# First layer's projections: context by itself, then five pairs of blocks as seven half-products

## The chip, the cores and the metric

One core of a Trainium2 chip runs the whole program. The time is that of the device for one execution, in microseconds (us); three runs were made of the kernel before, and one further execution was recorded by the profiler. TensorE (PE in the rows) multiplies matrices, ScalarE (ACT), VectorE (DVE) and GpSimd (POOL) work element by element, and SyncE (SP) and GpSimd issue the DMA transfers.

## The reference

Two layers of a backbone over 1024 latent tokens and 256 context tokens, width 1024. Each layer normalises and modulates its input, projects it with one matrix of 1024 x 3,488 columns, runs four groups on the parts (neighbourhood attention, latent attention with low rank, a token MLP, a short convolution), gates each, projects back and adds:

```python
hx = modulate(rms_norm(x, norm_g), sh_x, sc_x)        # latent, 1024 tokens
hc = modulate(rms_norm(ctx, norm_g), sh_c, sc_c)      # context, 256 tokens
(a_q, a_k, a_v, a_g, b_cq, b_ckv, b_kr, b_g,
 c_u, c_v, c_g, d_b, d_c, d_h, d_g) = jnp.split(hx @ w_in, IN_SPLIT_POINTS, axis=-1)
...
x_new = x + g_x * merge_branches((out_a, out_b, out_c, out_d), (a_g, b_g, c_g, d_g), w_out)
```

Context goes through the same weights. The last layer needs of context only the keys and values (`update_ctx` is false there). All is in float32.

## The kernel before

**Tiles.** Activations lie with channels on the partitions. Tokens come in three chunks (`CHUNKS`, L34): 0 and 1 are the latent tokens, 512 each, and 2 is context, 256. A projection block is 128 output columns; `BLOCKS` (L44) names them, two to most parts: cu, cg (token MLP), dc, dh, db, dg (convolution), ckv0, cq, ak, aq, bg, ag. A product in float32 is made of three matmuls in a faster format: every operand is split into a high part (a cast) and a low part (the rest), and `mm3` (L186) multiplies high by high, high by low, low by high. So a block over one chunk is 8 x 3 = 24 matmuls. Its weights come through `w_block` (L372): a DMA into a tile "wr", the cast on ScalarE into "wh" (L360), the subtraction on GpSimd into "wl" (L365). Each of the three tags has two tiles (`BUFS`, L122); "x" has 20, "g" 24.

**Order.** Code runs once to record instructions. A planner then orders each engine's instructions by when they are ready in its own estimate and by the order in which they were recorded, and gives out tiles as they come free. Between `pe.chain(True)` and `pe.chain(False)` TensorE's instructions keep their recorded order.

**Layer 0** uses `standard()` (L755): every block over all three chunks, with `proj` (L458), from cg to bg; then `ag` (L885) with the first parts of the latent attention (`mla_load`, `mla_keys`, `units[0].prep`) in between (L1437). After each `proj` one of the fillers runs, which compute the conditioning of both layers on VectorE (`mod_group_dve`, L331).

**Layer 1** uses `paired()` (L810). Two blocks of a part and the two latent chunks make a 2 x 2 by 2 x 2 product of half-blocks (4 of the 8 row groups each), computed with seven products in place of eight (`proj2`, L707; `product`, L698, is 12 matmuls of 512 columns). The sums of right-hand tiles are made once, on GpSimd and VectorE (`right_parts` L682, `right_sums` L691). The sums of weights are made for each pair, and each of the seven is split by `w_op` (L674) into one of four tiles, two "wh" and two "wl". The keys and values of context come before, in fixed order, with `av_tile` (L545) for the values and `ckv_steps` (L563) for the low-rank part.

## Time and profile before

| | |
|---|---|
| three runs | median 1477.39 us (1474.11 to 1480.54) |
| profiled execution | 1475.18 us, its span 1473.4 us |
| TensorE (matmul) | 1392.8 us busy, 95% of the span |
| TensorE (weight load) | 1170.5 us, 79% |
| VectorE | 860.6 us, 58% |
| ScalarE | 612.8 us, 42% |
| GpSimd | 499.3 us, 34% |
| granted TensorE clock, mean | 0.992 of full speed |
| DMA | 166.45 MB, mean 113 GB/s |

An engine's share is its busy time over the span. Matmuls overlap each other's ends, so the spacing of their starts tells more than their durations. The granted clock is 1.00 at 2.4 GHz and 0.50 at 1.2 GHz. Layer 0's projections run from about 25 to 448 us, its attention and output to about 815 us; layer 1's projections run to about 1141 us.

### The profile page before, as it was taken

How to read it: one execution, taken by the hardware profiler on the slowest of the kernel's cores; microseconds unless marked ns; L12 is line 12 of the kernel's file. 1: busy time of each engine (PE TensorE's matmuls, PEld its weight loads, DVE VectorE, ACT ScalarE, POOL GpSimd, SP SyncE). 2: the span in 40 equal slices, each digit the busy share in tenths (PEclk: the TensorE clock that was granted, in tenths of full speed). 3: DMA queues.
4: the chain of work that ended last, by engine and by line, in shares of the span. 5: the costliest groups of instructions: out<-in, count | busy, mean ns of one | idle time of the engine just before them, and what ended most of it. 6: DMA issues, size and time to landing. Idle time of an engine off the chain costs nothing. (4 is left out here: it accounts for less than half of the span.)

```text
span 1473.4 us, 23094 instructions
## 1 busy us (share of the span) xinstructions
PE 1392.8 (95%) x8844; PEld 1170.5 (79%) x8844; DVE 860.6 (58%) x1906; ACT 612.8 (42%) x1387; POOL 499.3 (34%) x403
## 2 busy tenths in 40 slices
PE   4999999999998999989999979989998999989997
PEld 2788888988887877678888869768886777778887
DVE  5966648064016777574564647666644777665574
ACT  5611111131226656563443413433443666555533
POOL 2154334032220000546613384633425001065641
PEclk9999999999999999999999999999999999999999
DMA  9513324355542002955433202420438102286241
GB/s 355 197 39 130 111 91 158 113 176 173 162 107 37 1 23 83 173 150 162 143 108 118 72 8 87 136 83 22 157 131 192 21 22 59 93 173 168 84 142 59
DMA packets 83822, 166.45 MB, mean 113 GB/s; under 512 B 8448, under 2 KB 35072, under 8 KB 83584
## 3 DMA queue, kind: packets, MB, share of 16 engines
q1 hardware_dynamic: 66688, 136.66, 28.0%
q0 software_dynamic: 15936, 27.27, 9.3%
q8 instruction: 69, 1.13, 0.3%
q10 hardware_dynamic: 1088, 1.05, 0.2%
q14 instruction: 41, 0.34, 0.1%
HBM read 135.33 MB, written 33.82 MB: 115 GB/s over the span
## 5 line engine op out<-in xcount | busy, mean ns | idle before, releaser
L173 PE MATMUL psb<-g,wh 128*128 128x512 f32 (+1 forms) x2152 | 582.1, 367 | 7.1 <-ACT tmp L730 1.5
L173 PEld LDWEIGHTS psb<-g,wh 128*128 128x128 f32 x2152 | 384.2, 189 | 81.8 <-ACT tmp L730 2.4
L173 PE MATMUL psb<-g,wl 128*128 128x512 f32 (+1 forms) x1256 | 414.8, 372 | 12.2 <-POOL wl L365 8.7
L173 PEld LDWEIGHTS psb<-g,wl 128*128 128x128 f32 x1256 | 237.7, 190 | 57.0 <-POOL wl L365 10.0
L365 POOL TENSOR_TENSOR wl<-wr,wh 128x1024 fp32r<-128x1024 f32 (+2 forms) x46 | 109.9, 2391 | 192.3 <-ACT wh L360 191.2
L173 PE MATMUL psb<-g,st 128*128 128x512 f32 (+1 forms) x616 | 161.2, 378 | 9.2 <-ACT wl L1063 3.7
L1046 DVE TENSOR_REDUCE s<-psb 128x1 f32<-128x512 f32 (+1 forms) x200 | 117.4, 590 | 68.5 <-PE psb L173 66.4
L173 PE MATMUL psb<-g,g 128*128 128x256 f32 (+1 forms) x784 | 129.1, 305 | 3.8 <-DMA g<-scr_ck 1.4
L173 PEld LDWEIGHTS psb<-g,st 128*128 128x128 f32 x616 | 97.0, 190 | 33.0 <-ACT g L1063 6.6
L173 PE MATMUL psv<-pt,g 128*64 128x256 f32 (+1 forms) x1312 | 119.4, 331 | 0.6 <-ACT pt L937 0.5
L937 ACT COPY pt<-pst 128x512 f32<-128x512 f32 x116 | 67.9, 586 | 110.7 <-PE pst L176 109.8
L173 PEld LDWEIGHTS psb<-g,g 128*128 128x128 f32 x784 | 105.2, 191 | 10.9 <-issue 2.9
L340 DVE CUSTOM_DVE_ANT_0 tmp<-g,x 128x512 f32<-128x512 f32 x112 | 94.4, 892 | 22.0 <-POOL x L473 20.3
L173 PEld LDWEIGHTS psv<-pt,g 128*64 128x64 f32 x1312 | 79.3, 137 | 32.4 <-issue 8.5
L176 PE MATMUL pst<-ident,g 128*128 128x128 f32 x448 | 79.1, 278 | 12.4 <-ACT g L1193 7.5
L935 DVE COPY pt<-pst 128x512 f32<-128x512 f32 x116 | 79.1, 683 | 10.3 <-PE pst L176 9.6
L360 ACT CAST wh<-wr 128x1024 fp32r<-128x1024 f32 (+2 forms) x47 | 43.2, 924 | 99.7 <-PE psb L173 70.2
L362 POOL TENSOR_SCALAR wh<-wr 128x1024 fp32r<-128x1024 f32 x16 | 44.4, 2772 | 106.5 <-PE pst L176 65.0
L1379 DVE SCALAR_TENSOR_TENSOR x<-psb,modG,x 128x512 f32<-128x512 f32 (+1 forms) x48 | 29.5, 615 | 85.7 <-PE psb L173 45.0
L176 PEld LDWEIGHTS pst<-ident,g 128*128 128x128 f32 x448 | 54.1, 140 | 29.5 <-ACT g L1193 10.3
L218 POOL TENSOR_TENSOR s<-s,mhalf 128x4 f32<-128x4 f32 (+4 forms) x22 | 35.1, 1595 | 80.9 <-DVE s L278 39.5
L1063 ACT ACTIVATE g<-psb,s,rq 128x512 f32<-128x512 f32 x64 | 49.2, 774 | 20.4 <-DVE s L1058 20.3
(246 smaller groups left out, 2142.3 us busy)
## 6 DMA issues: line engine op xcount, KB each, us to landing
g<-in_wmod SPq DMA_DIRECT2D x48, 512.0 KB, 4.7
wr<-in_wtb SPq DMA_DIRECT2D x28, 512.0 KB, 3.9
wr<-in_wout SPq DMA_DIRECT2D x27, 512.0 KB, 3.8
x<-in_wtb SPq DMA_DIRECT2D x40, 256.0 KB, 4.4
st<-in_nab SPq DMA_DIRECT2D x24, 384.0 KB, 3.4
x<-in_xT SPq DMA_DIRECT2D x32, 256.0 KB, 5.1
g<-scr_q POOLq DMA_DIRECT2D x32, 256.0 KB, 7.2
x<-x SPq DMA_DIRECT2D x24, 256.0 KB, 2.4
```

What stands on the lines that cost most here:

```text
L173: return self._next(nc.tensor.matmul(*p, **k))
L176: return self._next(nc.tensor.transpose(*p, **k))
L218: pool.tensor_tensor(r0, v, mhalf[:, :n], ALU.pow)
L340: dve.tensor_tensor_reduce(junk, w[:, hf * 512:hf * 512 + 512], crow[cond, hf], 1.0, 0.0, ALU.mult, ALU.add, part[:, i, cond, hf:hf + 1])
L360: act.copy(hi, raw)
L362: pool.tensor_scalar(hi, raw, 1.0, None, ALU.mult)
L365: (pool if lo_eng == "pool" else dve).tensor_tensor(lo, raw, f(hi), ALU.subtract)
L935: dve.tensor_copy(dst, src)
L937: act.copy(dst, src)
L1046: dve.reduce_max(st["mx"][:, i:i + 1], s_, AX.X)
L1063: act.activation(dst, sps[i], AF.Exp, bias=nb[:, 1:2], scale=rq[:, 0, tq:tq + 1], accum_out=self.rs[:, t, h, i:i + 1])
L1379: dve.scalar_tensor_tensor(xa, p, mod[l]["G"][:, fb, cond:cond + 1], xa, ALU.mult, ALU.add)
```

## The change

Layer 0 now runs `half_paired()`: `first_groups()` (the old code for cg, dc, dh, db, dg), then `value_blocks`, then five pairs by `proj2`: cq, ak, aq, bg and, after the branch of both layers, ag. `value_blocks` keeps a fixed order on TensorE: `ckv0` over chunks 2 and 1; the ten blocks cq, ak, aq, bg, ag over context alone, each with its own `w_block`; the values of context; `ckv0` over chunk 0; then the values of the latent tokens with the right-hand sums between them. `w_op` takes its tiles from three tags (six tiles) up to bg, and the differences of weights then lie in "x" instead of "wr". In `proj2` further work may be put ahead of any of its products (`mid`): in the last pair, ag, which now has a fixed order too, the loads of the latent attention stand ahead of the second product and its first keys ahead of the seventh; the preparation of the first queries comes after all seven. In layer 1 the weights of ak0 and ckv0 are asked for ahead of the tokens of chunk 1. Five of layer 0's fillers move up, so that all run in `first_groups`. In the neighbourhood attention one transposed tile in three is always copied by VectorE (for even `cb` it was ScalarE), and the context queries there lie in a tile "wr" instead of "st".

```diff
@@ -462,8 +462,9 @@
                 evac(c, p)
-            if fillers:
-                fillers.pop(0)()
+            for _ in range(2 if name in ("dc0", "db0", "dc1", "db1", "dg1") else 1):
+                if fillers:
+                    fillers.pop(0)()
@@ -528,9 +529,13 @@
         wcv = early.get(l) or w_tok(a["wcv"][l], 256)
+        ahead_w = {}
         for c in all_chunks:
             if l > 0:
                 cu(c)
+            if last and c == 1:
+                for n in ("ak0", "ckv0"):
+                    ahead_w[n] = w_block(a["wtb"][l, BLOCKS.index(n)])
             cv_tokens(c)
...
@@ -670,9 +675,10 @@
         nop = [0]
+        w_tags = ["wh", "wl", "wr"]
         def w_op(raw, lo_eng="pool"):
-            t = T(("wh", "wl")[nop[0] % 2], [2, 512], F32R)
+            t = T(w_tags[nop[0] % len(w_tags)], [2, 512], F32R)
             nop[0] += 1
@@ -704,55 +710,66 @@
-        def proj2(base, evac, mid=None):
+        def proj2(base, evac, mid={}, raw="x"):
             r = {}
             for j in range(2):
+                t = T("st", [2, 512]) if raw == "st" else None
                 for k in range(2):
-                    r[j, k] = T("x", [512])
+                    r[j, k] = T("x", [512]) if t is None else t[:, k]
                     sp.dma_start(r[j, k], a["wtb"][l, BLOCKS.index(f"{base}{j}")][:, k * 512:(k + 1) * 512])
-            q = T("wr", [2, 512])
+            qt = T("wr", [2, 512]) if "wr" not in w_tags else None
+            q = [T("x", [512]) if qt is None else qt[:, k] for k in range(2)]
             a11, a12 = w_op(r[0, 0]), w_op(r[0, 1])
-            dve.tensor_tensor(q[:, 1, :], r[0, 0], r[1, 0], ALU.subtract)
+            dve.tensor_tensor(q[1], r[0, 0], r[1, 0], ALU.subtract)
             dve.tensor_tensor(r[1, 0], r[1, 0], r[1, 1], ALU.add)
-            dve.tensor_tensor(q[:, 0, :], r[1, 0], r[0, 0], ALU.subtract)
-            dve.tensor_tensor(r[0, 1], r[0, 1], q[:, 0, :], ALU.subtract)
-            s2, s1 = w_op(q[:, 0, :], "dve"), w_op(r[1, 0])
-            x_, y_ = PS("b", [512]), PS("b", [512])
-            product(x_, a11, "11")
-            m1 = T("tmp", [512])
-            act.copy(m1, x_)
-            product(y_, a12, "21")
+            dve.tensor_tensor(q[0], r[1, 0], r[0, 0], ALU.subtract)
+            dve.tensor_tensor(r[0, 1], r[0, 1], q[0], ALU.subtract)
+            ops = {0: a11, 1: a12, 2: w_op(q[0], "dve"), 3: w_op(r[1, 0])}
+            later = {0: (4, q[1], "dve"), 2: (5, r[0, 1], "dve"), 3: (6, r[1, 1], "pool")}
+            x_, y_, z_ = PS("b", [512]), None, None
+            def step(n, p, name, first=True):
+                for fn in mid.get(n, []):
+                    fn()
+                product(p, ops[n], name, first)
+                if n in later:
+                    k, src, eng = later[n]
+                    ops[k] = w_op(src, eng)
+            def kept_copy(eng, p):
+                t = T("tmp", [512])
+                (eng.copy if eng is act else eng.tensor_copy)(t, p)
+                return t
+            step(0, x_, "11")
+            m1 = kept_copy(act, x_)
+            y_ = PS("b", [512])
+            step(1, y_, "21")
             dve.tensor_tensor(m1, y_, m1, ALU.add)
             evac(0, m1, 0)
-            s3 = w_op(q[:, 1, :], "dve")
-            product(x_, s2, "2", False)
-            u2 = T("tmp", [512])
-            act.copy(u2, x_)
-            s4 = w_op(r[0, 1], "dve")
+            step(2, x_, "2", False)
+            u2 = kept_copy(act, x_)
             z_ = PS("b", [512])
-            product(z_, s1, "1")
-            z5 = T("tmp", [512])
-            dve.tensor_copy(z5, z_)
-            if mid is not None:
-                mid()
-            a22 = w_op(r[1, 1])
-            product(x_, s3, "3", False)
+            step(3, z_, "1")
+            z5 = kept_copy(dve, z_)
+            step(4, x_, "3", False)
             dve.tensor_tensor(z5, x_, z5, ALU.add)
             evac(1, z5, 1)
-            product(z_, s4, "22", False)
+            step(5, z_, "22", False)
             dve.tensor_tensor(u2, z_, u2, ALU.add)
             evac(1, u2, 0)
-            product(x_, a22, "4", False)
+            step(6, x_, "4", False)
             evac(0, x_, 1)
         def block_c(name, c, evac):
-            hi, lo = w_block(a["wtb"][l, BLOCKS.index(name)])
+            hi, lo = ahead_w.get(name) or w_block(a["wtb"][l, BLOCKS.index(name)])
             p = PS("b", [CHUNKS[c][1]])
             mm3(p, [(hi[:, kc, :], lo[:, kc, :], hap(c, kc, 0), hap(c, kc, 1)) for kc in range(KC)])
             evac(c, p)
-        def standard():
+        def first_groups():
             cv_tail = [lambda: cv_gate(all_chunks[-1])]
@@ -789,23 +806,59 @@
-            wav = w_tok(a["wav"][l], 288)
-            for t in range(10):
+        def value_blocks(ctx_first):
+            wav = w_tok(a["wav"][l], 288, ("o", "o"), ("o", "o"))
+            pe.chain(True)
+            late = []
+            def ckv_block(c, hi, lo):
+                p = PS("b", [CHUNKS[c][1]])
+                mm3(p, [(hi[:, kc, :], lo[:, kc, :], hap(c, kc, 0), hap(c, kc, 1)) for kc in range(KC)])
+                late.append(ckv_steps(c, p))
+            def on():
+                for fn in [fns.pop(0) for fns in late if fns]:
+                    fn()
+            w = w_block(a["wtb"][l, BLOCKS.index("ckv0")])
+            ckv_block(2, *w)
+            ckv_block(1, *w)
+            for name, fn in ctx_first:
+                block_c(name, 2, fn)
+                on()
+            for t in (8, 9):
                 av_tile(t, wav)
+            ckv_block(0, *w)
+            parts = [right_parts(0), right_parts(1)]
+            for i in range(2):
+                right_sums(i, parts[i])
+            for t in (4, 5, 6, 7):
+                av_tile(t, wav)
+                on()
+            for i in range(2, 4):
+                right_sums(i, right_parts(i))
+            for t in range(4):
+                av_tile(t, wav)
+            pe.chain(False)
             av_windows()
-            proj("ckv0", (0, 1, 2), ckv_evac)
-            for j in range(2):
-                proj(f"cq{j}", all_chunks, lambda c, p: cq_evac(c, p, j))
+        def half_paired():
+            first_groups()
+            while fillers:
+                fillers.pop(0)()
+            evacs = {"cq": cq_evac, "ak": k_evac, "aq": lambda c, p, j: q_evac(c, p, j, 0.125),
+                     "bg": lambda c, p, j: act.activation(map_(2 + j, c), p, AF.Silu),
+                     "ag": lambda c, p, j: act.activation(map_(j, c), p, AF.Silu)}
+            value_blocks([(f"{n}{j}", lambda c, p, n=n, j=j: evacs[n](c, p, j)) for n in evacs for j in range(2)])
+            proj2("cq", evacs["cq"])
             kr = kr_rotate()
-            for j in range(2):
-                proj(f"ak{j}", (0, 1, 2), lambda c, p: k_evac(c, p, j))
-                if j == 0:
-                    cq_stats()
+            proj2("ak", k_evac)
             kr_transpose(*kr)
-            for j in range(2):
-                proj(f"aq{j}", all_chunks, lambda c, p: q_evac(c, p, j), scale=0.125)
-            for j in range(2):
-                proj(f"bg{j}", all_chunks, lambda c, p: act.activation(map_(2 + j, c), p, AF.Silu))
+            proj2("aq", evacs["aq"])
+            cq_stats()
+            w_tags.remove("wr")
+            proj2("bg", evacs["bg"])
@@ -820,7 +873,7 @@
-            w = w_block(a["wtb"][l, BLOCKS.index("ckv0")])
+            w = ahead_w["ckv0"]
             ckv_block(2, *w)
@@ -875,25 +928,14 @@
             cq_stats()
+            w_tags.remove("wr")
             proj2("bg", lambda c, p, j: act.activation(map_(2 + j, c), p, AF.Silu))
-        agw = []
-        def ag_weights():
-            agw.extend(w_block(a["wtb"][l, BLOCKS.index(f"ag{j}")]) for j in range(2))
-        def ag(c):
-            for j, (hi, lo) in enumerate(agw):
-                p = PS("b", [CHUNKS[c][1]])
-                mm3(p, [(hi[:, kc, :], lo[:, kc, :], hap(c, kc, 0), hap(c, kc, 1)) for kc in range(KC)])
-                act.activation(map_(j, c), p, AF.Silu)
+        ph = Phase("prj", ("o",))
         if last:
-            ph = Phase("prj", ("o",))
             paired()
         else:
-            standard()
-            ag_weights()
+            half_paired()
@@ -1205,7 +1247,7 @@
                 self.PT[n] = T("pt", [len(js), 128])
-                evac(self.PT[n], pt_, "DAD"[n] if self.cb % 2 else "DAA"[n])
+                evac(self.PT[n], pt_, "DAD"[n])
@@ -1273,7 +1315,7 @@
             def prep(self):
-                self.qd = T("st", [2, 2, 256], F32R)
+                self.qd = T("wr", [2, 2, 256], F32R)
                 for hl in range(2):
@@ -1429,18 +1471,11 @@
-        order = (0, 1) if last else (2, 0, 1)
-        if last:
-            proj2("ag", lambda c, p, j: act.activation(map_(j, c), p, AF.Silu), lambda: (mla_load(), mla_keys(0), units[0].prep()))
-            ph.close()
-        else:
-            for c in order[:-1]:
-                ag(c)
-                if c == 2:
-                    mla_load()
-            mla_keys(0)
-            units[0].prep()
-            ag(order[-1])
+        pe.chain(True)
+        proj2("ag", lambda c, p, j: act.activation(map_(j, c), p, AF.Silu), {1: [mla_load], 6: [lambda: mla_keys(0)]})
+        units[0].prep()
+        pe.chain(False)
+        ph.close()
         ph = Phase("att", ("pt", "pc"))
```

## Rows read from the trace of the kernel before

**Rows 1.** Busy time by stage: length, each engine's busy us (instructions), granted clock, DMA share, GB/s

```profile
64.00:254.00 190.00, 187.24 (x1120) 164.06 (x1119) 124.67 (x339) 35.05 (x57) 79.40 (x43) 0.99 0.33 112
...
286.00:420.00 134.00, 134.00 (x728) 114.99 (x727) 43.95 (x114) 32.63 (x55) 36.45 (x34) 1.00 0.44 146
...
925.00:1125.00 200.00, 192.31 (x826) 153.12 (x825) 118.33 (x156) 80.48 (x140) 85.24 (x77) 0.99 0.32 104
...
1125.00:1145.00 20.00, 15.88 (x78) 12.22 (x76) 9.21 (x17) 8.49 (x16) 7.93 (x12) 1.00 1.45 266
```

**Rows 2.** Timeline of TensorE in layer 0, 282 to 293 us: start, length, instructions

```profile
282.63 0.62 PE L173 MATMUL psb<-g,wh 128*128 128x512 f32 x2
...
291.69 0.62 PE L173 MATMUL psb<-g,wh 128*128 128x512 f32 x2
```

**Rows 3.** Timeline of ScalarE, both layers: casts of whole blocks, with their wait

```profile
327.43 1.05 ACT L360 CAST wh<-wr 128x1024 fp32r<-128x1024 f32 x1 [2.18 <-PE psb L173]
...
857.25 1.05 ACT L360 CAST wh<-wr 128x1024 fp32r<-128x1024 f32 x1 [2.38 <-PE psb L173]
```

**Rows 4.** Timeline of TensorE in layer 1, 857 to 870 us

```profile
857.12 0.40 PE L173 MATMUL psb<-g,wh 128*128 128x256 f32 x2
866.19 0.58 PE L173 MATMUL psb<-g,wl 128*128 128x256 f32 x1 [8.67 <-POOL wl L365]
...
867.21 0.63 PE L173 MATMUL psb<-g,wh 128*128 128x256 f32 x2
...
867.85 0.63 PE L173 MATMUL psb<-g,wh 128*128 128x256 f32 x2
...
869.38 0.28 PE L173 MATMUL psb<-g,wl 128*128 128x256 f32 x1
...
869.73 0.29 PE L173 MATMUL psb<-g,wl 128*128 128x256 f32 x1
```

**Rows 5.** Timeline of GpSimd in layer 1, 830 to 872 us

```profile
836.71 2.39 POOL L365 TENSOR_TENSOR wl<-wr,wh 128x1024 fp32r<-128x1024 f32 x1 [18.13 <-ACT wh L360]
...
846.94 16.90 POOL L687 TENSOR_TENSOR x<-g 128x512 f32<-128x512 f32 x12
863.80 2.34 POOL L365 TENSOR_TENSOR wl<-wr,wh 128x1024 fp32r<-128x1024 f32 x1
```

**Rows 6.** Busy time in two-microsecond windows around waits; the third number from the right is the clock

```profile
104.00:106.00 2.00, 0.92 (x10) 0.95 (x12) 2.00 (x14) 0.00 (x0) 2.00 (x1) 0.64 0.00 0
106.00:108.00 2.00, 2.00 (x22) 2.00 (x21) 1.02 (x5) 0.00 (x0) 1.22 (x2) 0.51 0.02 4
992.00:994.00 2.00, 1.88 (x5) 1.50 (x5) 2.00 (x3) 0.00 (x0) 1.77 (x2) 0.51 0.38 133
```

**Rows 7.** Timeline of TensorE: three of its waits

```profile
105.08 3.36 PE L173 MATMUL psb<-tmp,g 128*64 128x128 f32 x32 [2.76 <-DVE s L500]
...
933.64 2.59 PE L173 MATMUL psb<-g,wh 128*128 128x512 f32 x10 [1.50 <-DVE wh L365]
...
990.76 0.73 PE L173 MATMUL psb<-g,wl 128*128 128x512 f32 x2 [2.04 <-ACT wl L360]
```

**Rows 8.** Waits of TensorE in the whole span: us in total, times, longest

```profile
PE pst L176 <- ACT g L1193: 7.5, 14, 0.7
...
PE psb L173 <- ACT wl L360: 3.2, 2, 2.0
```

**Rows 9.** Timelines of GpSimd and of VectorE in layer 0, 249 to 255 us

```profile
251.20 2.94 POOL L365 TENSOR_TENSOR wl<-wr,wh 128x1024 fp32r<-128x1024 f32 x1 [1.89 <-ACT wh L360]
...
251.18 0.68 DVE L340 CUSTOM_DVE_ANT_0 tmp<-g,x 128x512 f32<-128x512 f32 x1
...
251.79 2.89 DVE L340 CUSTOM_DVE_ANT_0 tmp<-g,x 128x512 f32<-128x512 f32 x1
```

**Rows 10.** Timeline of VectorE in layer 1, 1133 to 1142 us: preparing the first queries

```profile
1138.91 0.69 DVE L1024 TENSOR_TENSOR tmp<-psb,tab 128x512 f32<-128x512 f32 x1 [4.09 <-PE psb L173]
1140.33 0.69 DVE L1029 TENSOR_TENSOR st<-tmp,st 128x512 fp32r<-128x512 f32 x1 [0.73 <-ACT st L1028]
```

More of the change, by code (lines that the diff above doesn't have):

```diff
@@ L628, in q_evac @@
             if scale != 1.0:
-                p, raw = T("tmp", [512]), p
+                p, raw = T("tmp", [n]), p
                 act.activation(p, raw, AF.Copy, scale=scale)
```

## The prediction, made before the result was known

> **What bounds the kernel now.** I first read the windows by stage. In layer 0's projections TensorE leaves no gap at all: busy for all of the stretch from 286 to 420 us, with VectorE, ScalarE and GpSimd each under a third of it [rows 1]. So there time is the number of matmuls times their spacing; an edit gains only by issuing fewer, and loses whatever wait it brings. TensorE's timeline gives the spacing: 39 matmuls of 512 columns between the two rows, (291.69 - 282.63) / 39 = 0.232 us each [rows 2]. Layer 1 already has seven half-products per pair, and its windows show the price: ten pairs from 925 to 1125 us leave TensorE idle for 200 - 192.3 = 7.7 us, about 0.8 us a pair, and the eleventh (the next 20 us) leaves 4.1 us [rows 1]. Then I read the weight path, because the change sends ten more whole blocks down it: ScalarE's casts, GpSimd's splits and the matmuls that wait for them [rows 3 to 5]. Last, what a wait does to the clock [rows 6, 7].
>
> **The change part by part.** All terms are added to the profiled execution's 1475.2 us (span 1473.4 and 1.8 around it).
>
> *Fewer matmuls.* A pair of blocks over the 1024 latent tokens is 2 x 2 x 24 = 96 matmuls of 512 columns; seven half-products are 7 x 12 = 84. Five pairs drop 60: 60 x 0.232 = -13.9 us. Context's 256-column matmuls are the same number as before, only moved.
>
> *Context's ten blocks by themselves.* This is the term that decides. `w_block` takes one "wh" and one "wl" tile, and there are two of each. In `value_blocks` the key/value block `ckv0` takes one pair of them and keeps it until its chunk 0, which stands in the fixed TensorE order behind all ten context blocks. So the ten share one pair of tiles. The rows show what a cast waits for: at 327.43 and at 857.25 ScalarE's cast starts when TensorE is through with the block that held the tile [rows 3]. At 857.25 that is one 256-column context block (ak0) giving its tile to ak1 while ckv0 holds the other one: just the state in which the ten blocks will be. The steady cycle follows from there. Without a wait the next block would start at 857.12 and reach its third matmul, the first that needs the low part, 0.24 us later, at 857.36. With one tile it needs the cast (1.05 us, from 857.25 to 858.30), some 0.08 us, the split of 128x1024 on GpSimd (2.39 us [rows 5]) and 0.05 us from the split's end to the matmul (863.80 + 2.34 against 866.19 [rows 4, 5]), so 860.82. That is 3.46 us late, against 24 x 0.118 = 2.8 us of work in the block. Before, a block covered this with 14 us of three chunks. Nothing covers it now: the order of TensorE's instructions is fixed there, and the pairs' own operands want the same tiles. cq0 is covered by ckv0's chunks 2 and 1 (some 8.4 us); the other nine pay: 9 x 3.46 = +31.1 us. The low end of this term is nothing, if tiles come free earlier than I read; that is a rival below.
>
> *The clock over this stretch.* A wait of 2.76 us before 105.08 and one of 2.04 us before 990.76 were each followed by 1.2 GHz (granted clock 0.51 in 106 to 108 and 992 to 994 us), while one of 1.50 us at 933.64 was not [rows 6, 7]. Each context block waits in two pieces, about 1.2 and 2.3 us, with two matmuls between. At 1.2 GHz a 256-column matmul takes 0.213 us (867.21 to 867.85 for three) instead of 0.118 (869.38 to 869.73) [rows 4]: 22 x 0.095 = 2.1 us a block, so between 0 and 9 x 2.1 = 18.9 us. I take a third, +6.3, since the pieces lie at both sides of the waits that were or were not followed by it.
>
> *Sums of the right-hand tiles on GpSimd.* 16 additions of some 1.3 us join the splits' queue; before, twelve of them stood ahead of one split and held it for 16.9 us [rows 5]. The gap of a cycle, 6.3 - 2.4 = 3.9 us, fits two or three. Between 0 and 16.9; I take +2, since x tiles are too few for more than seven to run at first.
>
> The row at 251.20 shows another thing: a split stretched to 2.94 us beside a VectorE reduction of two SBUF inputs that began 0.02 us earlier, and the next reduction held for 2.89 us [rows 9]. The Trainium skill ("SBUF — State Buffer", Who interferes with whom) says that VectorE and GpSimd share a port pair, held by one instruction as a whole, and that two SBUF inputs on VectorE count; the row agrees. By the rule alone every one of nine splits could wait out such a reduction, 9 x 0.55 = 5 us more as an estimate; I leave it out.
>
> *Five pairs in layer 0.* The operand waits of layer 1, 0.77 us a pair [rows 1]: +3.9, from 0 to twice that. Besides, "x" has 20 tiles and 15 are held (ten maps, two for context's gates, three square sums); a pair that also keeps its differences in "x" needs six, and the rotated keys two more. So the second pair (ak) must wait for the small key transposes and `cq_stats` to free some. Between 0 and about 6 us (a landing, four operand steps); +2.
>
> *Fillers.* Five are moved up: 5 x 8 reductions of 0.68 us [rows 9] = 27 us more for VectorE in 64 to 254 us, where it has 124.7 of 190 [rows 1]. It still fits under TensorE: 0, and up to 5 if it holds a PSUM tile back.
>
> *Layer 1.* ckv0's split stood behind the twelve sums and TensorE waited 8.67 us, then ran some 14 matmuls at the slow spacing (1.3 us) [rows 4, 5]. `ahead_w` is meant for it, but its tiles still come free only after chunk 1's cu, as before. Between -10 and 0; -5. Six operand tiles in place of four: between all 7.7 us of idle time in the ten pairs [rows 1] and none; waits for the casts of "wl" alone are 3.2 us [rows 8]. Half: -3.8. The end of the last pair: loading the latent attention's operands at its second product takes the 4.1 us [rows 1] off, but the queries' preparation now comes after all seven; multiply, cast and subtract lie between 1138.91 and 1141.02 [rows 10], 2.1 us, exposed in layer 1 and for a part in layer 0. Between -4 and +4; -1.3.
>
> *Transposed tiles on VectorE instead of ScalarE*, and the context queries' tile from another tag: TensorE waited 7.5 us for ScalarE's exponentials in these stages [rows 8]; -3 to +2, 0 taken.
>
> Sum: -13.9 + 31.1 + 6.3 + 2 + 3.9 + 2 + 0 - 5 - 3.8 - 1.3 + 0 = +21.3, so 1496.5 us. The median of the runs shown is 2.2 us above the profiled execution, the lowest 1.1 below it; I forecast 1496.
>
> **The rivals.** *Context's blocks don't queue for one tile.* If the casts run ahead (a tile freed earlier, or another one used), the 31.1 and the 6.3 go and the rest gives 21.3 - 37.4 = -16.1: 1459 us, faster. For it speaks that every cast before was hidden under matmuls [rows 1, 3]; against it that each waited for the block two before, which is possible only with two tiles. It decides at about 1 us a block: with 9 us in place of 37.4 the kernel is just 0.5% faster. *Gain and wait cancel.* The blocks queue, but the clock holds, the sums stay out of the way, and layer 1 loses its 10 us wait and all 7.7: -13.9 + 31.1 + 3.9 + 2 - 10 - 7.7 - 4 = +1.4, 1477 us. *The clock stays low.* All nine blocks at 1.2 GHz and two or three splits behind sums: +12.6 and +6 on the forecast, 1515 us or more.
>
> **How the numbers follow.** My forecast has 0.52, with 1485 to 1512 as its own range; the low clock 0.14, no queue 0.21, cancelling 0.13. With 0.5% (7.4 us, about what a measurement of this kernel can tell from no change) as the bound: faster 0.21, same 0.13, slower 0.66. The sum of the low ends is 1475.2 - 13.9 + 31.1 - 10 - 7.7 - 4 - 3 = 1468, of the high ends about 1550. The range reaches over cancelling and part of the two outer rivals: 1461 to 1517.
>
> **What would show it.** After the last gate of the short convolution, TensorE should show ten blocks of 24 matmuls, nine with a wait of some 2.3 us before the third matmul, put down to GpSimd's "wl", and one of 1.1 before the first, put down to the cast; the way from the first to the last context block should be about 60 us instead of 28, with a granted clock under 1 in places. The pairs should start some 20 us apart (84 x 0.232 = 19.5 and a wait). In layer 1 the wait for "wl" before ckv0 shows whether loading ahead did anything. The prediction is wrong if the context blocks stand 2.8 us apart, or if their casts start before the block ahead of them ends.

## The result, and the profile after

The changed kernel takes 1534.99 us (median of 4 runs, 1531.37 to 1536.50) against 1478.52 us of the kernel before: ratio 1.0379, 95% interval 1.0362 to 1.0395. It is slower, as forecast, but 39 us beyond the forecast of 1496 and outside the range of 1461 to 1517. The profiled execution took 1531.37 us, with a span of 1529.6 against 1473.4 us before.

Four times of each trace cut the difference into stages: layer 0's first exponential table load on ScalarE (its projections are over), TensorE's wait for the first gelu of layer 1 (1.4 us in every trace), the gate's table load in layer 1's first pair, and layer 1's exponential table load.

| stage (us) | before | after | difference |
|---|---|---|---|
| start to layer 0's attention | 448.26 | 498.66 | +50.4 |
| layer 0's attention and output, to layer 1's first gelu | 388.9 | 387.8 | -1.1 |
| layer 1: latent block, value tiles, start of the first pair | 94.4 | 97.8 | +3.4 |
| layer 1: pairs | 210.2 | 212.5 | +2.3 |
| layer 1's attention to the end | 331.6 | 332.8 | +1.2 |

So layer 0's projections hold nearly all of it. The windows of the changed kernel there and in layer 1, as in [rows 1] (length, each engine's busy us, granted clock, DMA share, GB/s):

```profile
64.00:250.00 186.00, 183.24 (x1092) 160.15 (x1092) 145.78 (x393) 34.73 (x56) 81.13 (x43) 0.99 0.41 137
262.00:333.00 71.00, 40.89 (x203) 37.10 (x203) 21.16 (x24) 15.06 (x26) 34.91 (x20) 0.71 0.27 86
333.00:376.00 43.00, 42.09 (x293) 40.84 (x293) 24.00 (x33) 12.14 (x25) 23.44 (x17) 0.97 0.19 61
376.00:498.00 122.00, 111.57 (x492) 88.82 (x490) 64.39 (x90) 49.66 (x88) 56.13 (x62) 0.96 0.58 166
984.00:1197.00 213.00, 198.49 (x853) 158.04 (x852) 112.35 (x154) 80.76 (x141) 91.80 (x86) 0.98 0.41 116
```

Before, TensorE had no gap from 262 to 448 us. Now the context blocks (262 to 333) leave it idle for 30.1 of 71 us, and what it does runs at a mean clock of 0.71; the value tiles (333 to 376) lose little; the pairs (376 to 498) leave 10.4 us. Busy time times (1 - clock) is an estimate of what the low clock costs: 11.9 + 1.3 + 4.5 = 17.7 us. Waits of 30.1 + 0.9 + 10.4 and this clock, less 13.9 us of matmuls, make 45 of the 50.4 us; 5 are not itemised (in part they are modelled ends: the two matmuls ahead of a split's wait count 0.50 us as busy, where two in a row take 0.24). The first window, in which five fillers were moved up, has no new wait. Layer 1's pairs (the last row) leave 14.5 of 213 us, where [rows 1] has 11.8 of 220; the longest wait there is new (TensorE's timeline):

```profile
990.36 5.53 PE L173 MATMUL psb<-g,wl 128*128 128x512 f32 x16 [3.10 <-POOL wl L365]
```

One context block on TensorE's timeline, with its two waits (start, length, instructions, [idle before <- what ended it]):

```profile
282.29 0.28 PE L173 MATMUL psb<-g,wl 128*128 128x256 f32 x1
283.63 0.50 PE L173 MATMUL psb<-g,wh 128*128 128x256 f32 x2 [1.06 <-ACT wh L360]
286.05 0.58 PE L173 MATMUL psb<-g,wl 128*128 128x256 f32 x1 [1.92 <-POOL wl L365]
286.43 0.63 PE L173 MATMUL psb<-g,wh 128*128 128x256 f32 x2
286.85 0.41 PE L173 MATMUL psb<-g,wl 128*128 128x256 f32 x1
287.07 0.63 PE L173 MATMUL psb<-g,wh 128*128 128x256 f32 x2
...
290.69 0.41 PE L173 MATMUL psb<-g,wl 128*128 128x256 f32 x1
292.07 0.50 PE L173 MATMUL psb<-g,wh 128*128 128x256 f32 x2 [0.96 <-ACT wh L360]
```

Three matmuls take 0.64 us (286.43 to 287.07), the 0.213 us of [rows 4] at 1.2 GHz: in this block all but the first few, after waits of no more than 1.92 us. Nine blocks wait; only the first of the ten is covered, as the prediction had it. Eight of the nine run half or more of their 24 matmuls at this spacing. One, after waits of 0.41 and 1.93 us, does not: three take 0.35 us there (272.30 to 272.65).

```profile
269.64 0.50 PE L173 MATMUL psb<-g,wh 128*128 128x256 f32 x2 [0.41 <-ACT wh L360]
272.07 0.39 PE L173 MATMUL psb<-g,wl 128*128 128x256 f32 x1 [1.93 <-POOL wl L365]
272.30 0.40 PE L173 MATMUL psb<-g,wh 128*128 128x256 f32 x2
272.53 0.28 PE L173 MATMUL psb<-g,wl 128*128 128x256 f32 x1
272.65 0.40 PE L173 MATMUL psb<-g,wh 128*128 128x256 f32 x2
```

The ninth waits longer, and GpSimd's timeline shows why (TensorE's wait last):

```profile
316.82 2.34 POOL L365 TENSOR_TENSOR wl<-wr,wh 128x1024 fp32r<-128x1024 f32 x1 [6.05 <-ACT wh L360]
319.12 10.45 POOL L693 TENSOR_TENSOR x<-g 128x512 f32<-128x512 f32 x7
329.52 2.80 POOL L365 TENSOR_TENSOR wl<-wr,wh 128x1024 fp32r<-128x1024 f32 x1
332.38 0.58 PE L173 MATMUL psb<-g,wl 128*128 128x256 f32 x1 [7.39 <-POOL wl L365]
```

Seven additions for the right sides stand ahead of the last split, and TensorE waits 7.39 us for it. The same happens in layer 1, where loading `ckv0` ahead left the picture of [rows 5] as it was, and TensorE's wait went from 8.67 to 9.96 us:

```profile
897.59 16.80 POOL L693 TENSOR_TENSOR x<-g 128x512 f32<-128x512 f32 x12
914.35 2.33 POOL L365 TENSOR_TENSOR wl<-wr,wh 128x1024 fp32r<-128x1024 f32 x1
916.74 0.58 PE L173 MATMUL psb<-g,wl 128*128 128x256 f32 x1 [9.96 <-POOL wl L365]
```

In the pairs, the longest wait is the second pair's (ak), 5.64 us for the cast of an operand whose raw weights landed late (ScalarE's timeline, then TensorE's):

```profile
403.31 0.62 ACT L360 CAST wl<-x 128x512 fp32r<-128x512 f32 x1 [3.86 <-DMA x<-in_wtb]
403.98 1.22 PE L173 MATMUL psb<-g,wl 128*128 128x512 f32 x2 [5.64 <-ACT wl L360]
```

### The profile page after: what moved, and what is told of

Its sections match the earlier page's. It is cut to its first block, busy times and chain, and to the rows that moved or that the text cites. A ratio compares the mean times of both kernels' runs of the same rounds, so it can differ in the third digit from the quotient of the medians.

```text
span 1529.6 us, 23255 instructions
## 1 busy us (share of the span) xinstructions
PE 1404.1 (92%) x8784; PEld 1176.0 (77%) x8784; DVE 947.6 (62%) x1999; ACT 645.2 (42%) x1438; POOL 567.6 (37%) x449
## 5 line engine op out<-in xcount | busy, mean ns | idle before, releaser
L173 PE MATMUL psb<-g,wh 128*128 128x512 f32 (+1 forms) x1886 | 510.1, 371 | 16.6 <-ACT wh L360 11.1
L173 PE MATMUL psb<-g,wl 128*128 128x512 f32 (+1 forms) x1144 | 373.4, 379 | 44.3 <-POOL wl L365 36.2
L173 PEld LDWEIGHTS psb<-g,wh 128*128 128x128 f32 x1886 | 346.0, 197 | 83.0 <-ACT wh L360 14.2
L173 PEld LDWEIGHTS psb<-g,wl 128*128 128x128 f32 x1144 | 224.8, 197 | 87.5 <-POOL wl L365 39.1
L173 PE MATMUL psb<-g,st 128*128 128x512 f32 (+1 forms) x600 | 159.6, 383 | 10.4 <-ACT wl L1105 3.7
L365 POOL TENSOR_TENSOR wl<-wr,wh 128x1024 fp32r<-128x1024 f32 (+1 forms) x46 | 111.5, 2425 | 149.1 <-ACT wh L360 147.9
L340 DVE CUSTOM_DVE_ANT_0 tmp<-g,x 128x512 f32<-128x512 f32 x112 | 96.8, 915 | 13.5 <-POOL x L474 11.8
L173 PE MATMUL psb<-g,wr 128*128 128x512 f32 (+1 forms) x490 | 98.1, 346 | 6.9 <-DMA g<-scr_cq 2.7
L173 PEld LDWEIGHTS psb<-g,wr 128*128 128x128 f32 x490 | 76.9, 190 | 20.0 <-ACT wr L360 3.9
L360 ACT CAST wh<-wr 128x1024 fp32r<-128x1024 f32 (+1 forms) x41 | 40.3, 985 | 117.0 <-PE psb L173 67.9
```

The costliest lines, as they stand in the source:

```text
L173: return self._next(nc.tensor.matmul(*p, **k))
L340: dve.tensor_tensor_reduce(junk, w[:, hf * 512:hf * 512 + 512], crow[cond, hf], 1.0, 0.0, ALU.mult, ALU.add, part[:, i, cond, hf:hf + 1])
L360: act.copy(hi, raw)
L365: (pool if lo_eng == "pool" else dve).tensor_tensor(lo, raw, f(hi), ALU.subtract)
```

## The experiments

Theory: the nine waits and the clock that falls in them are the loss. Rivals: the sums, the pairs' operands, layer 1. "Stage" below is the start of layer 0's attention in the profile (448.26 before, 498.66 after). Every time stands beside runs of the kernel before on the same chip.

### The queue for one pair of tiles

**own_tiles**: the operands of the latent block (`ckv0`) in tiles of another kind.

```
-            w = w_block(a["wtb"][l, BLOCKS.index("ckv0")])
+            w = w_block(a["wtb"][l, BLOCKS.index("ckv0")], tags=("g", "g"))
```

> The changed kernel with one edit: the first layer's latent block, whose operands the third and last of its chunks still needs after the ten context blocks, keeps them in two tiles of another kind, so the ten blocks take turns on two pairs of tiles. Theory 1 (the ten wait for one pair, and TensorE's clock falls in those waits): the ten waits of about 3 us and most of the 1.2 GHz time go, the stretch from the first context block to the first pair shortens by 35 to 45 us, the run takes 1490 to 1500 us. A rest of up to 0.8 us a block may stay, because a block's raw tile is filled by a transfer of 3.8 us and two raw tiles take turns. Theory 2 (the loss is in the seven half-products of the pairs, in the sums or in the second layer): less than 10 us is gained, 1525 to 1535 us.

Measured 1517.56 us (ratio 1.0275, 1.0255 to 1.0295), stage 485.8. Between the two theories: the queue goes, but only 17 us come back. TensorE's waits from 240 to 500 us in that run (us in total, times, longest):

```profile
PE pst L176 <- DVE s L223: 11.4, 3, 7.1
PE psb L173 <- ACT wl L360: 5.5, 1, 5.5
PE psb L173 <- POOL g L365: 4.4, 1, 4.4
PE psb L173 <- POOL wl L365: 3.5, 3, 1.9
```

The splits' 22.5 us are down to 3.5 (and 4.4 for the latent block's own, whose cast and split came behind cq0's), and a new wait stands on top: the latent block's reciprocal roots, whose power is taken on GpSimd behind the additions.

**filled_waits**: the queue stays, the gaps are filled.

```
+            for _ in range(0 if last else 24):
+                pe.matmul(p, hap(0, 0, 0)[:, :128], hap(c, 0, 0), start=True, stop=True)
```

> The changed kernel with one edit: ahead of each of the first layer's ten context blocks TensorE runs 24 extra matmuls of 256 columns, whose results are thrown away; at 0.118 us each they fill 2.8 us of the wait for the one pair of operand tiles. The queue for the pair stays as it is. Theory 1a (a good part of the loss is the clock: the blocks' own matmuls run at 1.2 GHz, 0.213 us apart instead of 0.118, because TensorE stands still between them): the blocks come about 6.4 us apart instead of 7.8, the run gains 10 to 17 us, 1518 to 1525 us. Theory 1b (only the queue counts: cast, split and matmuls in a ring): no gain, 1530 to 1545 us, since the extra matmuls add to a ring that is already full.

Measured 1526.53 us (1.0331, 1.0314 to 1.0348), stage 493.3. The blocks come 6.4 us apart, as expected, instead of 7.8; the window over them:

```profile
262.00:319.00 57.00, 54.46 (x447) 53.25 (x445) 13.79 (x20) 14.82 (x25) 27.55 (x16) 1.00 0.32 107
```

The clock is 1.00 throughout. The gain is 8.5 us by the medians and 7 by the two ratios, a little under the expectation; 5.3 us of it lie in this stage. The 240 extra matmuls fit into the waits, and what they gain is the clock's share. The wait for the last split (7.2 us) stayed.

### GpSimd's order, and the order on TensorE

**split_first**: `after` puts the additions behind the last split in both layers.

```
-            parts = [right_parts(0), right_parts(1)]
+            parts = [right_parts(0, w_last[0]), right_parts(1, w_last[0])]
...
```

> The changed kernel with one rule for GpSimd's queue: the additions that prepare the half-products' right sides stand behind the last weight split that TensorE waits for (the tenth context block's in the first layer, the latent block's in the second). Nothing else moves. If the two longest waits of TensorE for a split (7.4 us in the first layer, 10.0 us in the second) are the price of that order, 5 go in the first layer and 8 to 10 in the second, and the run takes 1519 to 1524 us. If the additions are themselves what the next stage waits for, they come 2.4 us late in each layer and the gain is given back: 1530 to 1537 us.

Measured 1542.36 us (1.0438, 1.0420 to 1.0456), slower than the change. Both long waits for a split went (in layer 0 the longest left is 1.9 us), and TensorE now waited for the roots: 4.8 us in layer 0 and 13.1 us in layer 1, since the additions got between split and root. **before_roots_first** puts them behind the last root (`pw[0]`), in layer 1 of the kernel before:

```
-            parts = [right_parts(0)]
...
-            parts.append(right_parts(1))
+            parts = [right_parts(0, pw[0]), right_parts(1, pw[0])]
```

> The kernel before with one rule for GpSimd's queue in the second layer: the additions for the right sides stand behind the last of the latent block's reciprocal roots (and so behind its weight split). Before, twelve of them (16.9 us) stood ahead of the split, and TensorE waited 8.7 us. If that order alone made the wait, the run gains 6 to 9 us, 1468 to 1472 us. If the additions then come too late for the first pair, the wait moves there: 1475 to 1482 us.

Measured 1474.73 us (0.9977, 0.9967 to 0.9988): the 8.7 us wait is gone, 2.7 us are gained, and waits of 5.5 and 2.1 us for VectorE's key copies took most of its place. So order alone gains little; that the two engines are short of time there is a reading, which before_parts_vector (below) bears out.

**latent_before** finishes the latent block ahead of the ten, behind value tiles 8 and 9.

```
+            for t in (8, 9):
+                av_tile(t, wav)
+                on()
+            ckv_block(0, *w)
             for name, fn in ctx_first:
                 block_c(name, 2, fn)
                 on()
-            for t in (8, 9):
-                av_tile(t, wav)
-            ckv_block(0, *w)
...
-                on()
```

> The changed kernel with the fixed order of TensorE changed in the first layer: the latent block's last chunk goes ahead of the ten context blocks, with two value tiles in front of it, so that its pair of operand tiles comes free for them, and its reciprocal roots are taken on GpSimd before the additions for the right sides are. Theory: the queue for one pair goes, as with tiles of its own (18 us gained there), and so do the 7.1 and 1.6 us that TensorE waited there for the roots, and the late start of the latent block there (4.4 and 2.3 us): 1500 to 1507 us. Up to 0.8 us a block stays, from two raw tiles at 3.8 us a transfer. Rival (the additions on GpSimd now hold the pairs themselves): above 1512 us, with a wait at the first pair's third product.

Measured 1508.76 us (1.0210, 1.0188 to 1.0231), stage 475.0: 26 us come back. What is left is at the first pair: 4.5 and 3.8 us for casts, and 5.5 us at the second. **alternate** (one context block, one value tile, and so on, still one pair of tiles; the additions come in the gaps between the splits and `cq_stats` behind the first pair):

```
+            for n, t in enumerate((8, 9, 4, 5, 6, 7, 0, 1, 2, 3)):
+                if n == 2:
+                    ckv_block(0, *w)
+                block_c(ctx_first[n][0], 2, ctx_first[n][1])
+                av_tile(t, wav)
+                on()
...
```

> The changed kernel with the first layer's ten context blocks and ten value tiles in turn on TensorE, one of each, GpSimd's additions for the right sides in the gaps between the splits, and the query statistics early as in the run beside this one. Still one pair of operand tiles for the ten blocks. Theory: a value tile's 24 matmuls of 288 columns (3.2 us) fill the 3 us that the next block waits for the pair, so the ten waits and the 1.2 GHz stretch go with no tile added; what may come is a wait of up to 8 us at the first pair, whose right sides are ready later against TensorE. 1485 to 1497 us. Rival (the ring of cast, split and block is no shorter than block and value tile together, or the additions stretch it): waits of 1 us and more at every block stay, above 1505 us.

Measured 1508.45 us (1.0209, 1.0180 to 1.0238), stage 476.9. No wait of 0.5 us or more for a context block's split is left: a value tile of 3.2 us in between covers cast and split. But 6.1 us for a VectorE copy, 8.4 and 2.1 us at the first pair and 3.9 us for GpSimd's addition of the squares come in their place.

### The sums

Two variants now end alike. In latent_before VectorE is busy for 36.0 and GpSimd for 38.2 of the 40 us from 310 to 350. GpSimd's timeline there:

```profile
320.73 1.75 POOL L365 TENSOR_TENSOR g<-x,g 128x512 fp32r<-128x512 f32 x1
322.44 1.75 POOL L693 TENSOR_TENSOR x<-g 128x512 f32<-128x512 f32 x1
324.14 1.75 POOL L365 TENSOR_TENSOR g<-x,g 128x512 fp32r<-128x512 f32 x1
325.86 3.44 POOL L693 TENSOR_TENSOR x<-g 128x512 f32<-128x512 f32 x2
```

and VectorE's there:

```profile
322.96 3.48 DVE L700 TENSOR_TENSOR x<-x,x 128x512 f32<-128x512 f32 x2
326.37 1.78 DVE L365 TENSOR_TENSOR g<-x,g 128x512 fp32r<-128x512 f32 x1
```

One operation in 1.7 us on each engine, two in 1.7 us together. **latent_sums_vector** gives all of them to VectorE in layer 0.

```
-                pool.tensor_tensor(t[k], f(H[c, kc][:, 0, :]), f(H[c, kc][:, 1, :]), ALU.add)
+                (pool if last else dve).tensor_tensor(t[k], f(H[c, kc][:, 0, :]), f(H[c, kc][:, 1, :]), ALU.add)
...
-                split(r[:, 0, :], r[:, 1, :], t[o], lo_eng="dve" if name in "12" else "pool")
+                split(r[:, 0, :], r[:, 1, :], t[o], lo_eng="dve" if name in "12" or not last else "pool")
```

> The kernel of latent_before (1509 us) with one edit: the first layer's 16 additions for the right sides and the remainders of its sums run on VectorE alone, not on VectorE and GpSimd. In latent_before both engines were full from 310 to 350 us, where an operation of 512 columns took 1.7 us on either, against 0.6 to 0.7 us on VectorE alone and 1.3 us on GpSimd alone: 48 of them took 40 us, past the end of the value tiles. Theory (the two slow each other, and that holds up the first pair): 48 at 0.62 us are 30 us, the first pair's waits of 4.5 and 3.8 us go, 8 to 14 us are gained: 1495 to 1501 us. Rival (the first pair waits for its raw weights, which find no tile, or for their casts): less than 4 us, 1505 us and above.

Measured 1494.19 us (1.0118, 1.0095 to 1.0141), stage 463.2: 14.6 us, just above the theory's 8 to 14. VectorE's timeline there:

```profile
322.32 2.49 DVE L365 TENSOR_TENSOR g<-x,g 128x512 fp32r<-128x512 f32 x4
324.73 0.68 DVE L700 TENSOR_TENSOR x<-x,x 128x512 f32<-128x512 f32 x1
...
326.03 2.49 DVE L693 TENSOR_TENSOR x<-g 128x512 f32<-128x512 f32 x4
```

Four in 2.41 us: alone, VectorE does one in 0.60 us, faster than the two engines together (0.85). The first pair's waits fall from 4.5 and 3.8 to 1.1 and 0.6 us.

The pace is not all that changed. First addition and last remainder in latent_before, on GpSimd:

```profile
310.22 10.56 POOL L693 TENSOR_TENSOR x<-g 128x512 f32<-128x512 f32 x7
346.60 6.86 POOL L365 TENSOR_TENSOR o<-x,o 128x512 fp32r<-128x512 f32 x4
```

and in latent_sums_vector, on VectorE:

```profile
301.65 8.64 DVE L693 TENSOR_TENSOR x<-g 128x512 f32<-128x512 f32 x7
341.37 1.95 DVE L365 TENSOR_TENSOR o<-x,o 128x512 fp32r<-128x512 f32 x2 [1.21 <-ACT o L360]
```

On GpSimd the additions stand behind the last context split (307.91 to 310.26 us); on VectorE they start 8.6 us earlier. From first to last it is then 41.7 us, with VectorE waiting for casts in between, against 43.2. So the sums are ready 10 us earlier, and most of that is the earlier start. No run separates the two, so how much of the 14.6 us the slower operations cost is not shown.

**no_right_sums** leaves the sums out, on another base (latent_before_raw, next):

```
-            parts = [right_parts(0), right_parts(1)]
-            for i in range(2):
-                right_sums(i, parts[i])
+            for i in range(4):
+                R["11", i], R["21", i], R["22", i] = H[0, i], H[0, i + 4], H[1, i + 4]
+                R["1", i], R["2", i], R["3", i], R["4", i] = H[1, i], H[1, i + 4], H[0, i], H[0, i + 4]
```

> The kernel of latent_before_raw without the first layer's right-side sums: the half-products take plain quarters of the activations where they took sums and differences, so 16 additions on GpSimd (24 us), 16 subtractions, 16 casts and 16 remainders are left out. It shows what those cost in time. If they are hidden behind the value tiles, no more than 2 us is gained on the run beside it. If GpSimd's queue and the tiles that they hold keep the pairs waiting, 8 to 15 us go. With them out of the way the first layer's gain by 60 fewer matmuls (13.9 us) should show against the kernel before, less what the ten blocks still wait: 1475 to 1485 us.

Measured 1517.50 us (1.0272, 1.0246 to 1.0298), only 4 below its neighbour. The first pair had no wait, but three of 7.1, 3.6 and 7.2 us stood at the pairs behind it, and its base has long waits of its own. It doesn't give the price of the sums.

### Raw weights, tiles and queues

**latent_before_raw**:

```
-            proj2("cq", evacs["cq"])
+            proj2("cq", evacs["cq"], raw="st")
```

and the same for ak and aq.

> The kernel of latent_before with one edit: the raw weights of the first layer's first three pairs are loaded into the two evacuation tiles instead of four of the twenty 512-column tiles, so that no more than nineteen of those are held at once. Theory 1 (the waits of 4.5 and 3.8 us at the first pair and of 5.5 us at the second come from raw weights that find no tile): they go with the 1.2 GHz stretches behind them, 12 to 18 us are gained on 1509, 1491 to 1497 us. Theory 2 (the first pair waits for the right sides, which GpSimd and VectorE finish late): the wait moves to the first pair's third product and less than 5 us is gained, 1504 us and above.

Measured 1521.50 us (1.0299, 1.0277 to 1.0320), 13 us worse than latent_before, with waits of 6.0 us at the first pair, 6.8 at the second and 3.7 and 1.6 at the third. A miss for both theories. Probably the raw weights and the evacuations held each other up in those tiles (the second pair's loads stand behind four spills on SyncE until 374.5 us); no run isolates it. **stats_early** moves `cq_stats` behind the first pair:

```
             proj2("cq", evacs["cq"])
+            cq_stats()
...
             proj2("aq", evacs["aq"])
-            cq_stats()
```

> The changed kernel with one step moved: the first layer's query statistics, which hold three of the twenty 512-column tiles, come straight behind the first pair instead of behind the third. Theory 1 (TensorE's wait of 5.6 us at the second pair, and the 1.2 GHz stretch behind it, come from a shortage of those tiles, which lets the pair's raw weights arrive late): 6 to 10 us are gained, 1525 to 1529 us. Theory 2 (the operand is late because VectorE and ScalarE have other work ahead of it): less than 2 us, 1533 to 1536 us.

Measured 1535.28 us (1.0388, 1.0369 to 1.0407), nothing. The 5.6 us wait went; 4.0 us for GpSimd's addition of the squares stood in its place. **latent_sums_vector_four** has four operand tiles (the diff of layer1_four_tiles, below) and one more 512-column tile, "xp", in the projections' pool:

```
-            sq = T("tmp" if second else "x", [512])[:, :n]
+            sq = T("tmp" if second else "xp" if c == 2 else "x", [512])[:, :n]
```

> The kernel of latent_sums_vector with four operand tiles for the half-products in both layers (the differences of the raw weights then sit in the third kind of tile and leave two 512-column tiles free) and one more 512-column tile for the projections. Six tiles cost 6.6 us in the second layer (layer1_alone against layer1_four_tiles), so 6 to 7 us should go there; in the first layer the wait of 5.5 us at the second pair goes if it is a shortage of 512-column tiles, with 4 us of low clock behind it: 10 to 17 us in all, 1480 to 1489 us. If that wait stays, 5 to 7 us in all.

Measured 1494.23 us (1.0114, 1.0099 to 1.0129): no gain, and the wait at the second pair is still 5.3 us, so a shortage of tiles was not the reason. SyncE's timeline in latent_sums_vector names another (a spill, a load of raw weights):

```profile
353.66 10.12 SPq L544 DMA_DIRECT2D scr_cq<-st  x3
363.83 0.46 SPq L720 DMA_DIRECT2D x<-in_wtb  x1
```

The second pair's load stands behind three spills of the first, each of which waits for VectorE. **latent_vector_spills** issues those spills from ScalarE, and moves layer 1's additions to VectorE:

```
+        def spill_act(dst, src):
+            (sp if last else act).dma_start(dst, src)
```

> The kernel of latent_sums_vector (1494 us) with two edits in different layers. First layer: the spills of the query-latent and key blocks are issued from ScalarE's queue, not from SyncE's, where three of them (353.7 to 363.8 us) stood ahead of the second pair's raw weights and waited for VectorE; if that order makes TensorE's wait of 5.5 us at the second pair, the wait goes with the low clock behind it and the first layer's stage ends 7 to 9 us earlier. Second layer: the 16 additions on VectorE, which alone took 12 us from the kernel before; the wait of 10.0 us for the latent block's split goes. Together 1473 to 1478 us. If the raw weights are late for want of a tile, the wait stays and the run takes 1481 to 1485 us.

Measured 1489.35 us (1.0077, 1.0059 to 1.0096), the best form of the change that was run. The wait fell from 5.5 to 3.4 us, not to nothing: the load is in time now, and the cast waits in ScalarE's queue behind the first pair's last evacuations. In layer 1 the expectation failed: the wait of 10 us went, but one of 4.1 us for the roots came, and its two stages took 307.5 us against 309.7 in latent_sums_vector.

### Layer 1, and the kernel before

**layer1_alone** calls the kernel before's `standard` and `ag` in layer 0:

> The changed kernel with the first layer's projections as they were before the change: no context blocks by themselves, no pairs, no second filler there. What stays is the second layer's share of the change (six operand tiles, a fixed order of its last pair, its latent block's weights cast ahead) and the small edits of the attention. By the terms of the prediction this is 9 us below the kernel before, 1469 us. By the trace of the changed kernel, which reaches the second layer 51 to 53 us late and ends 56 us late, the second layer's share and the attention's gain nothing and may lose up to 5 us: 1478 to 1484 us. If it is above 1490 us, the loss of the change is not in the first layer's projections.

Measured 1482.52 us (1.0037, 1.0024 to 1.0051): layer 1's share of the change, with the attention's small edits, costs 5 us where 9 were to be gained. **layer1_four_tiles** takes the third kind of operand tile away:

```
-        w_tags = ["wh", "wl", "wr"]
+        w_tags = ["wh", "wl"]
```

> The kernel of layer1_alone (first layer as before, second layer as changed) with four operand tiles for the half-products instead of six, as in the kernel before. If the six tiles themselves cost the 5 us (a new wait of 3.1 us for a split at the second pair and a later start of each operand behind them), the run is back at 1476 to 1479 us. If the cost is in the fixed order of the last pair, the latent weights cast ahead or the attention's small edits, it stays at 1481 to 1485 us.

Measured 1475.92 us (0.9989, 0.9971 to 1.0006): with four tiles the 5 us are gone. With the changed layer 0 ahead of it the same edit did less, in **change_four_tiles** (on the changed kernel) and **latent_raw_four** (on latent_before_raw):

> The changed kernel with four operand tiles for the half-products in both layers and nothing else. The second layer alone gained 6.6 us by it. If the first layer's pairs behave likewise and the wait at their second pair (5.6 us) is a shortage of 512-column tiles, two of which this edit frees, 10 to 17 us are gained, 1518 to 1525 us; if the first layer has no use of it, 1528 us.

Measured 1533.18 us (1.0366, 1.0344 to 1.0388), 1.8 us, not clear of the spread of either kernel's runs.

> The kernel of latent_before_raw with four operand tiles in both layers. If the six tiles cost 5 us in the second layer and bring nothing in the first, it ends 5 us below the run beside it: 1486 to 1492 us. If the first layer's pairs need six tiles (operands asked for two products ahead), it ends 3 us or more above it.

Measured 1516.36 us (1.0253, 1.0222 to 1.0285), 5 us. The four comparisons gave 6.6, 1.8, 5.1 and (latent_sums_vector_four) 0 us: six tiles never helped, but what they cost is not settled. Layer 1's pairs took from 207 to 217 us over the runs, and their end waits between nothing and 4.3 us for a DMA.

**before_parts_vector**: the kernel before, with layer 1's 16 additions on VectorE (in the line of latent_sums_vector, `dve if last else pool`).

> The kernel before with one edit in the second layer: the 16 additions for the right sides run on VectorE, which stood idle from 859 to 874 us, and not on GpSimd, where twelve of them (16.9 us) stood ahead of the latent block's split. The wait of 8.7 us for that split falls to about 3 us, and the roots that wait in GpSimd's queue come earlier as well: 5 to 8 us gained, 1469 to 1473 us. If the additions hold up VectorE's own steps of the normalisation, nothing is gained: 1476 to 1482 us.

Measured 1465.53 us (0.9917, 0.9901 to 0.9933), better than expected. VectorE and GpSimd there:

```profile
846.21 11.94 DVE L687 TENSOR_TENSOR x<-g 128x512 f32<-128x512 f32 x16
```

```profile
845.24 3.81 POOL L218 TENSOR_TENSOR s<-s,mhalf 128x16 f32<-128x16 f32 x1 [4.07 <-DVE s L504]
849.02 2.56 POOL L365 TENSOR_TENSOR wl<-wr,wh 128x1024 fp32r<-128x1024 f32 x1
860.46 2.40 POOL L365 TENSOR_TENSOR wl<-wr,wh 128x1024 fp32r<-128x1024 f32 x1 [8.87 <-ACT wh L360]
```

The split ran at 849 us, not at 864 [rows 5], and no wait for it is left; layer 1's first stage took 84.2 instead of 94.4 us. Two things changed here as well: the split has no additions ahead of it, and an addition takes 0.75 us on VectorE (11.94 for sixteen) where it took 1.41 on GpSimd (16.90 for twelve). **before_sums_vector** moves the remainders too:

> The kernel before with the second layer's additions and also all remainders of its sums on VectorE; GpSimd keeps the weights' splits. In before_parts_vector (1466 us) only the additions were moved. If VectorE has room for eight more operations of 0.6 us and they go faster without GpSimd beside them, 1462 to 1466 us; if VectorE is then late with the first pair's operands, 1467 to 1471 us.

Measured 1465.22 us (0.9908, 0.9893 to 0.9922): the same within the interval. Both beat the kernel before and the change, and neither has anything of the change in it.

## Why the prediction was wrong

*Fewer matmuls, -13.9.* No run isolates it. In the best form run of the change, layer 0's stage still ends at 458.6 us, 10.3 behind the kernel before: what it brings in waits is more than what it saves.

*Context's ten blocks, +31.1: the mechanism was right, the near agreement in part luck.* Nine wait, the first doesn't, before the third matmul and all but one of them before the first as well, 30.1 us together. 5.5 of these belong to the sums, which held up the last block's split (7.39 us instead of some 1.9); the other eight blocks wait 2.7 us each where 3.46 were counted. The cycle of cast, split and block was counted well: in filled_waits, at a clock of 1.00, the blocks come 6.4 us apart, 3.6 more than their 2.8 of work.

*The clock, +6.3 of 18.9: the step that failed first.* "I take a third" was wrong: 11.9 us, nearly two thirds of 18.9, fell on the context blocks. Another 1.3 on the value tiles and 4.5 on the pairs had no term at all; together they are 17.7 by the windows. The pieces are 1.06 and 1.92 us and most blocks repeat them; [rows 6, 7] showed single waits of 1.50 and 2.04 us, and a single one of 1.50 us without consequence said nothing of a row of them. filled_waits shows the clock's part apart from the queue (1.00 instead of 0.71, 8.5 us). The rival "the clock stays low", at 0.14, came nearest: its 1515 us or more holds, though not every block ran at 1.2 GHz and only one split stood behind the sums.

*Sums on GpSimd, +2 of 16.9: mis-sized, and its place was missed.* Standing ahead of the last split they cost about 5.5 us there (a wait of 7.39 instead of some 1.9). A larger part is hidden behind the queue: once that is gone, the 48 operations on VectorE and GpSimd take 43 us, beside 26 us of value tiles (eight at 3.2), and the first pair waits. Moving them to VectorE gained 14.6 us (latent_sums_vector), by an earlier start and by quicker operations, which no run separates. The prediction left out the stretching of [rows 9], "5 us more as an estimate". The Trainium skill ("SBUF — State Buffer", Who interferes with whom) has a VectorE instruction with two SBUF inputs and a GpSimd instruction that reads SBUF exclude each other, one holding the shared ports at a time; the runs agree: 0.60 us alone on VectorE, 1.7 us on each of the two when they alternate.

*Five pairs and "x", +3.9 and +2.* Waits in the pairs were 10.4 us: 4.8 beside the second pair's 5.6, so the first term is near. The second was short (5.6 for 2) and had the wrong cause: with tiles to spare the wait stayed (latent_sums_vector_four); with the spills off SyncE's queue it fell to 3.4 us, and what is left stands in ScalarE's queue (latent_vector_spills).

*Fillers, 0: right.* TensorE is idle for 2.8 us in the first window, as before [rows 1].

*Layer 1, -5, -3.8 and -1.3: the other step that failed.* Measured +3.4 and +2.3. `ahead_w` moved nothing: the latent block's cast starts 5.9 us into the stage (5.7 before), probably since its tiles come free no earlier, and its split stayed behind twelve additions, as the prediction itself had read in [rows 5] and yet paid half for: TensorE's wait there rose from 8.67 to 9.96 us. Six tiles saved nothing: a new wait of 3.10 us stands at the second pair. At the last pair 2.7 us of waits for the attention's transfers are left of 3.8, where all 4.1 were to go, and the queries' preparation adds 1.5.

So 19 of the 35 us between sum (+21.3) and measurement (+56.2 by the spans) lie in layer 0, 11.4 of them the clock; 16 lie behind layer 0's projections, nearly all in layer 1. With no queue the 1459 us of that rival would not have come: own_tiles, latent_before and latent_sums_vector show three limits one behind the other, the operand tiles, the engines and queues that make the sums, the queue of loads and casts. Open are 5 us of layer 0's stage, the size and the cause of the six tiles' cost, and a form of the change in which all three limits are lifted; it was not found.

## What to carry to other kernels

A block that loses its long neighbours needs its cast and split covered by something: count tiles that an earlier block still holds, and put other work between, or the waits come in a row; here the clock fell with them. Don't price the low clock behind a repeated short wait by what a single one did: here two thirds of the most that it could cost came, where a third was taken. When two engines do elementwise work on the same stretch, look at the duration of one operation with the other engine idle, and at what stands in each engine's queue: here moving 16 additions from GpSimd to VectorE made the kernel before 0.8% faster, more than any part of the change. And an order that lifts one wait can make the next: split_first removed both waits that it was made for and was slower.

## What was not expected of the hardware

Work added to a waiting TensorE made the kernel faster, by 8.5 us by the medians: the clock stayed at 1.00 over the context blocks, where it had been 0.71. Two engines were slower than one, operation for operation: 512 columns took 1.7 us on VectorE and on GpSimd while both worked, 0.85 us an operation between them, and 0.60 us back to back on VectorE by itself. And after waits of 1.06 and 1.92 us, in turn, blocks ran half or more of their matmuls at 1.2 GHz, where a single wait of 1.50 us had no such stretch behind it [rows 7].
